# A Conformer convolution in a four-module trunk: the filters' tap products queued behind the norm's root, the gate kept in PSUM, and TensorE's filters half a tile later

## The chip, the cores and the metric

The kernel runs on one core of one Trainium2 chip. A core has five engines, each with its own instruction queue that is worked through in order: TensorE (PE; its weight loads are listed as PEld), VectorE (DVE), ScalarE (ACT), GpSimd (POOL) and SyncE (SP), which here issues nearly all DMAs. Engines wait for each other by semaphores. TensorE writes its products to PSUM, eight banks of 128 x 512 fp32; everything else lies in SBUF. The metric is the device time of one execution in microseconds (us), as a median of runs.

## What is computed

The trunk has two layers; each is a half-step SwiGLU FFN, a mixer, a second half-step FFN and a gated per-layer embedding, each behind an RMS norm. The mixer of layer 0 is the Conformer convolution, that of layer 1 a sparse attention. The change touches the convolution and the last norm.

```python
def rms_norm(x, g):
    return x * lax.rsqrt(jnp.mean(x * x, axis=-1, keepdims=True) + RMS_EPS) * g

def conformer_conv(h, w_pw1, b_pw1, w_dw, b_dw, ln_g, ln_b, w_pw2, b_pw2):
    u = h @ w_pw1 + b_pw1
    a, g = jnp.split(u, 2, axis=-1)
    u = a * jax.nn.sigmoid(g)
    u = lax.conv_general_dilated(u, w_dw[:, None, :], window_strides=(1,),
        padding=[(CONV_KERNEL - 1, 0)], feature_group_count=D_MODEL, ...) + b_dw
    mu = jnp.mean(u, axis=-1, keepdims=True)
    var = jnp.mean(jnp.square(u - mu), axis=-1, keepdims=True)
    u = jax.nn.silu((u - mu) * lax.rsqrt(var + LN_EPS) * ln_g + ln_b)
    return u @ w_pw2 + b_pw2

for i in range(DEPTH):                      # DEPTH = 2
    x = x + 0.5 * swiglu(rms_norm(x, ffn1_norm[i]), ...)
    h = rms_norm(x, mix_norm[i])
    x = x + (conformer_conv(h, ...) if i == 0 else nsa_mixer(h, ...))
    x = x + 0.5 * swiglu(rms_norm(x, ffn2_norm[i]), ...)
    x = x + jax.nn.sigmoid(rms_norm(x, ple_norm[i]) @ ple_w_gate[i]) * (p[i] @ ple_w_in[i])
return rms_norm(x, final_norm)
```

There are 512 tokens of 1024 channels; the filter has 31 taps and runs over each channel by itself.

## The kernel before

The activations lie transposed: eight tiles of 128 channels by 512 tokens. A weight block is 128 x 128, and eight blocks make a unit of 128 x 1024. SP loads a unit (`raw`), ACT copies it to a rounded half (`wh`, L230), and VectorE or GpSimd subtracts to get the rest (`wl`, L231). There are two `raw` buffers and five of `wh` and of `wl`, so a split waits until TensorE has done with the unit five before it. Each product is three matmuls, high by high, high by low, low by high (`mm3`, L254 to L256), of 512 columns.

An RMS norm's factor is not waited for. The products run on unnormalized activations; meanwhile TensorE sums squares over channels (L338), VectorE adds epsilon (`v`, L387), GpSimd takes the root (`r`, L331), TensorE spreads it over the partitions by four transposes (L363), and ACT copies it to `R` (L370). VectorE multiplies each product by `R` as it takes it out of PSUM.

The convolution (`conv`) goes over tiles c = 0 to 7. For each tile TensorE makes two groups of 24 matmuls: `pa` for the value, then `pg` for the gate. `glu` multiplies the gate by `R` (L538), has ACT take the sigmoid (L539), multiplies the value by `R` (L540) and multiplies both (L544, or L550 where the filter isn't TensorE's). The filter of tile 0 runs on ACT and GpSimd (L578, L579), those of tiles 1 and 2 on VectorE (62 steps over two PSUM banks, L563 and L565), those of tiles 3 to 7 on TensorE. For these:

- `taps` (L528) has GpSimd multiply the tap weights `dw`, a small load on SP, by a mask: four products `tw` of 128 x 1152 for each tile. The loop asks for them two tiles ahead (`TAPS_AT`), and there are buffers for two tiles.
- the gated tile goes to DRAM and comes back in another order (`ud` and `uu`, L545 and L546 on SP),
- TensorE runs 36 small matmuls over `uu` and `tw` (`dw_pe`, L636), ACT takes the result out (L641), and two more DMAs (`yd`, L642 and L643) bring it to its final order.

Where TensorE's filters stand between the groups is written out by hand. `PE_LATE` names the filters that run two tiles behind, after `pa` of the later tile; the others run after the loop. `centre` (L604 and after) forms a mean from the first four filtered tiles. Then come the products of the per-layer embedding, 16 "z tiles" of 6 matmuls each (`z_tiles`, ACT takes them out at L474), which fill TensorE while the layer norm is worked out; `FILL` says how many stand where: the last entry ahead of the remaining filters, the first ahead of the sums over all tiles (L722), the next two ahead of the second root's transposes, the rest behind them. Then VectorE and ACT normalize the tiles (L741 to L745) and TensorE multiplies them by `w_pw2`.

The last stage (`final`) works in two halves of 256 tokens. The last three tiles of the embedding's gate (`late`) run for half 0, then for half 1: product, times `R` (L1222), sigmoid (L1223), times z (L1224), add (L1225), square (L1227). `norm` has two steps for each half: sums and root, then transposes, ACT's copy (L1197), eight scalings on VectorE and GpSimd (L1206, L1204) and the output DMAs (L1208). `NORM_AT` places the two steps of half 0 at the second and third tile of half 1.

A scheduler orders what the code issues on each engine by its own estimate of time, within what the data and buffers allow, so an engine's order isn't simply that of the code.

## Time and profile before

| | |
|---|---|
| median of 3 runs (lowest to highest) | 2115.72 us (2115.25 to 2117.07) |
| the profiled execution's own time | 2116.84 us |
| its span in the profile | 2115.1 us |
| the convolution's groups, filters and z tiles | about 371 to 553 us |
| mean granted clock of TensorE over the span | 0.99 |

The profile shows one execution. A row of the timeline gives start, length, engine, line, operation, tile written and tiles read, and in brackets how long the engine stood idle just before and what ended that. `x8` means that eight like instructions are merged in the row. A row of the waits gives who waited for whom, the sum in us, how often, and the longest. PEclk is the share of full speed that TensorE was granted.

### The profile page before, as it was taken

The page shows a single profiled execution, that of the slowest core. Times are in us where ns is not written, and L with a number is a line of the kernel's source. Part 1 is how long each engine was busy: PE and PEld are TensorE (multiplying, and loading weights), DVE is VectorE, ACT ScalarE, POOL GpSimd, SP SyncE. Part 2 cuts the span into 40 slices and gives each one's busy share as a digit, 9 for nine tenths or more (in the row PEclk, how much of TensorE's full clock was granted, in tenths as well). Part 3 has the DMA queues.
Part 4 walks back from the last instruction along what each step waited for, and adds up shares of the span by engine and source line. Part 5 has one row for each costly group of instructions (what it writes and reads, how often), then busy time and mean ns, then how long its engine had stood idle before and what let it go on. Part 6 is the DMA issues. An engine that isn't in the chain of part 4 may idle for free. (4 is left out here: it accounts for less than half of the span.)

```text
span 2115.1 us, 25526 instructions
## 1 busy us (share of the span) xinstructions
PE 2067.5 (98%) x9608; PEld 1715.7 (81%) x9608; DVE 966.9 (46%) x1744; ACT 830.1 (39%) x1394; POOL 1030.9 (49%) x646
## 2 busy tenths in 40 slices
PE   9999999899999999999999999999999999999997
PEld 7888888688788888888788888888888778888887
DVE  5330334497635303335532133346989753213334
ACT  5322224552624222234432223326888642222333
POOL 2444443675435444444444444556666444444442
PEclk9999999999999999999999999999999999999998
DMA  5323323233463232233223322453232033223322
GB/s 171 94 96 100 100 93 100 69 127 105 154 183 126 98 100 94 96 100 115 93 98 100 99 92 98 156 174 116 83 91 95 33 123 98 93 99 100 96 94 75
DMA packets 77323, 223.30 MB, mean 106 GB/s; under 512 B 8624, under 2 KB 16592, under 8 KB 77200
## 3 DMA queue, kind: packets, MB, share of 16 engines
q1 hardware_dynamic: 76208, 219.26, 32.5%
q0 software_dynamic: 848, 2.34, 0.3%
q8 instruction: 76, 1.25, 0.2%
q14 instruction: 47, 0.39, 0.1%
q10 hardware_dynamic: 144, 0.07, 0.0%
HBM read 203.25 MB, written 16.29 MB: 104 GB/s over the span
## 5 line engine op out<-in xcount | busy, mean ns | idle before, releaser
L231 POOL TENSOR_TENSOR wl<-raw,wh 128x1024 fp32r<-128x1024 f32 x311 | 778.1, 2503 | 866.4 <-ACT wh L230 862.3
L230 ACT ACTIVATE wh<-raw 128x1024 fp32r<-128x1024 f32 (+1 forms) x331 | 348.9, 1056 | 932.9 <-PE b L255 833.3
L254 PE MATMUL b<-s,wh 128*128 128x512 f32 x1728 | 676.0, 392 | 4.8 <-ACT s L308 3.5
L255 PE MATMUL b<-s,wh 128*128 128x512 f32 x1728 | 674.6, 390 | 1.9 <-DVE s L309 1.6
L256 PE MATMUL b<-s,wl 128*128 128x512 f32 x1728 | 674.0, 390 | 0.0
L254 PEld LDWEIGHTS b<-s,wh 128*128 128x128 f32 x1728 | 325.4, 188 | 74.5 <-ACT s L308 5.7
L255 PEld LDWEIGHTS b<-s,wh 128*128 128x128 f32 x1728 | 325.3, 188 | 70.1 <-DVE s L309 3.0
L256 PEld LDWEIGHTS b<-s,wl 128*128 128x128 f32 x1728 | 325.1, 188 | 67.5
L254 PE MATMUL b<-hid,wh 128*128 128x512 f32 x704 | 273.9, 389 | 0.0
L256 PE MATMUL b<-hid,wl 128*128 128x512 f32 x704 | 273.2, 389 | 0.0
L255 PE MATMUL b<-hid,wh 128*128 128x512 f32 x704 | 273.2, 389 | 0.0
L411 DVE TENSOR_TENSOR t<-b,R 128x512 f32<-128x512 f32 x88 | 60.7, 690 | 348.2 <-PE b L256 348.2
L415 DVE TENSOR_TENSOR hid<-t,hid 128x512 fp32r<-128x512 f32 x88 | 173.2, 1970 | 55.4 <-ACT hid L414 55.2
L451 DVE SCALAR_TENSOR_TENSOR s<-b,s 128x512 f32<-128x512 f32 x64 | 44.3, 692 | 326.5 <-PE b L256 326.5
L254 PEld LDWEIGHTS b<-hid,wh 128*128 128x128 f32 x704 | 132.1, 188 | 27.6
L255 PEld LDWEIGHTS b<-hid,wh 128*128 128x128 f32 x704 | 132.1, 188 | 27.4
L256 PEld LDWEIGHTS b<-hid,wl 128*128 128x128 f32 x704 | 132.1, 188 | 27.4
L409 DVE TENSOR_TENSOR t<-b,R 128x512 f32<-128x512 f32 x88 | 60.7, 690 | 158.0 <-PE b L256 94.6
L1032 POOL TENSOR_SCALAR e<-e,sm,gates 128x512 f32<-128x512 f32 (+3 forms) x96 | 61.1, 642 | 40.8 <-DVE sm L1026 35.1
L414 ACT ACTIVATE hid<-t 128x512 fp32r<-128x512 f32 x88 | 55.4, 631 | 54.0 <-DVE t L412 54.0
L412 DVE TENSOR_TENSOR t<-t,t 128x512 f32<-128x512 f32 x88 | 68.5, 782 | 8.0 <-ACT t L410 0.2
L308 ACT ACTIVATE s<-s,small 128x512 fp32r<-128x512 f32 x48 | 38.0, 798 | 76.5 <-DVE s L451 34.5
(223 smaller groups left out, 2265.8 us busy)
## 6 DMA issues: line engine op xcount, KB each, us to landing
raw<-in_w SPq DMA_DIRECT2D x335, 512.0 KB, 3.5
skew<-table SPq DMA_DIRECT2D x16, 320.0 KB, 9.6
z<-t SPq DMA_DIRECT2D x16, 256.0 KB, 2.3
z<-z SPq DMA_DIRECT2D x16, 256.0 KB, 3.4
tt<-skew SPq DMA_DIRECT2D x16, 256.0 KB, 2.8
wr<-in_w SPq DMA_DIRECT2D x8, 512.0 KB, 3.8
q<-t SPq DMA_DIRECT2D x32, 128.0 KB, 2.4
s<-in_xT SPq DMA_DIRECT2D x8, 256.0 KB, 5.5
```

The lines of the kernel that those rows point to most:

```text
L230: self.nc.scalar.activation(h[:, c], t[:, c], AF.Copy)
L231: eng.tensor_tensor(l[:, c], t[:, c], h[:, c].bitcast(F32), op=OP.subtract)
L254: mm(out, sh, mh, start=start, stop=False)
L255: mm(out, sh, ml, start=False, stop=False)
L256: mm(out, sl, mh, start=False, stop=stop)
L409: nc.vector.tensor_tensor(gr, pg, R, op=OP.mult)
L411: nc.vector.tensor_tensor(ur, pu, R, op=OP.mult)
L412: nc.vector.tensor_tensor(ur, ur, gr, op=OP.mult)
L414: nc.scalar.activation(h, ur, AF.Copy)
L415: nc.vector.tensor_tensor(l, ur, h.bitcast(F32), op=OP.subtract)
L451: nc.vector.scalar_tensor_tensor(self.xs[m], p, 0.5, self.xs[m], op0=OP.mult, op1=OP.add)
L1032: nc.gpsimd.tensor_scalar(dst, dst, sm[:, a, bi:bi + 1], gate, op0=OP.mult, op1=OP.mult)
```

## The change

```diff
-PE_LATE = (3, 4, 5, 6)
+PE_LATE = (3, 4, 5)
...
-FILL = (6, 0, 4, 0)
+FILL = (6, 0, 4, 3)
...
     def rsqrt(self, v, n):
         y = self.tiny.tile([128, 4], F32, name="r", tag="r")[:, :n]
-        self.nc.gpsimd.tensor_tensor(y, v, self.power[:, :n], op=OP.pow)
+        self.root = self.nc.gpsimd.tensor_tensor(y, v, self.power[:, :n], op=OP.pow).ins
         return y
...
     def glu(self, c, pa, pg):
         nc, R = self.nc, self.R
-        tg, ta = self.tmp(), self.tmp()
+        tg, ta = pg, self.tmp()
...
         for c in range(KD):
             for t in TAPS_AT.get(c, ()):
-                self.T[t] = self.taps(t)
+                with self.tc.issue_after(self.root):
+                    self.T[t] = self.taps(t)
...
-                if p is pa and c - 2 in PE_LATE:
+                if p is pg and c - 2 in PE_LATE:
                     drain(queues["pe"].pop(0))
...
-                if h == 1 and m - late[0] in NORM_AT:
+                if h == 1 and m == late[1]:
                     next(norms[0])
```

The tap products may be issued only behind the latest root. `glu` multiplies the gate by `R` within its PSUM bank, ACT's sigmoid works there too, and L544 or L550 reads it there, so that the bank is held until then. The filters of tiles 3, 4 and 5 run after `pg` instead of `pa` of the tile two later; filter 6 runs right behind filter 5, and three z tiles stand ahead of filter 7. In the last stage only the first step of half 0's norm stands within half 1; the second follows behind all of half 1's tiles. Behind line 675 the changed kernel's line numbers are higher by one.

GpSimd's queue at the start of the convolution, a piece of the difference (- before, + changed; rows that differ in buffer numbers alone count as different):

```order
+L543 MEMSET uu_3072 128x4x8
+L331 TENSOR_TENSOR r<-v,power 128x4
 L528 TENSOR_TENSOR tw_2639<-bd,dw_2637 128x1152
 L528 TENSOR_TENSOR tw_2641<-bd,dw_2637 128x1152
 L528 TENSOR_TENSOR tw_2643<-bd,dw_2637 128x1152
 L528 TENSOR_TENSOR tw_2645<-bd,dw_2637 128x1152
-L528 TENSOR_TENSOR tw_2752<-bd,dw_2750 128x1152
-L528 TENSOR_TENSOR tw_2754<-bd,dw_2750 128x1152
-L528 TENSOR_TENSOR tw_2756<-bd,dw_2750 128x1152
-L528 TENSOR_TENSOR tw_2758<-bd,dw_2750 128x1152
-L331 TENSOR_TENSOR r<-v,power 128x4
-L579 TENSOR_TENSOR y_2694<-y_2694,t_2696 128x512
```

The root moved from behind the eight tap products of tiles 3 and 4 to ahead of them.

TensorE behind the last group of tile 7 (`b_3395` before, `b_3388` changed), first before, where L636 of `b_3557` is filter 6 and of `b_3598` filter 7:

```order
L256 MATMUL b_3395<-s_2549,wl_3188 128x512
L604 MATMUL b_3520<-sum_3170,meanr 128x512
L338 MATMUL b_3524<-meanr,sum_3170 128x1 x4
L636 MATMUL b_3557<-uu_3388,tw_2974 128x128 x9
L636 MATMUL b_3557<-uu_3388,tw_2976 128x128 x9
L636 MATMUL b_3557<-uu_3388,tw_2978 128x128 x9
L636 MATMUL b_3557<-uu_3388,tw_2980 128x128 x9
L636 MATMUL b_3598<-uu_3512,tw_3085 128x128 x9
```

and changed, where `b_3454` is filter 5, `b_3510` filter 6 and `b_3590` the first z tile:

```order
L256 MATMUL b_3388<-s_2549,wl_3142 128x512
L636 MATMUL b_3454<-uu_3230,tw_2860 128x128 x9
L636 MATMUL b_3454<-uu_3230,tw_2862 128x128 x9
L636 MATMUL b_3454<-uu_3230,tw_2864 128x128 x9
L636 MATMUL b_3454<-uu_3230,tw_2866 128x128 x9
L636 MATMUL b_3510<-uu_3381,tw_2970 128x128 x9
L636 MATMUL b_3510<-uu_3381,tw_2972 128x128 x9
L636 MATMUL b_3510<-uu_3381,tw_2974 128x128 x9
L636 MATMUL b_3510<-uu_3381,tw_2976 128x128 x9
L604 MATMUL b_3553<-sum_3124,meanr 128x512
L338 MATMUL b_3557<-meanr,sum_3124 128x1 x4
L254 MATMUL b_3590<-zp_3237,wh_3262 128x512
```

Filter 5 moved from ahead of tile 7's gate group to behind it, filter 6 ahead of the centre, and z tiles (three) to between the centre and filter 7. Further on, GpSimd's order has three weight differences (L231) between the last sum of squares (L623) and the second root, where it had two.

VectorE near the end of the program, where `t` and `s` are tile 7 of half 1, the `hid` rows scale half 0 for the output, and the second `v` is half 1's; before:

```order
L1192 TENSOR_SCALAR v<-b_16099 128x2
L1222 TENSOR_TENSOR t_16168<-b_16119,R 128x256
L1206 SCALAR_TENSOR_TENSOR hid_16149<-s_12199,small,b_16144 128x256
L1206 SCALAR_TENSOR_TENSOR hid_16154<-s_12203,small,b_16144 128x256
L1206 SCALAR_TENSOR_TENSOR hid_16154<-s_12205,small,b_16144 128x256
L1206 SCALAR_TENSOR_TENSOR hid_16158<-s_12209,small,b_16144 128x256
L1206 SCALAR_TENSOR_TENSOR hid_16163<-s_12211,small,b_16144 128x256
L1224 TENSOR_TENSOR t_16168<-t_16168,z_15941 128x256
L1225 TENSOR_TENSOR s_12213<-s_12213,t_16168 128x256
L1192 TENSOR_SCALAR v<-b_16175 128x2
```

and changed:

```order
L1193 TENSOR_SCALAR v<-b_16091 128x2
L1223 TENSOR_TENSOR t_16136<-b_16111,R 128x256
L1225 TENSOR_TENSOR t_16136<-t_16136,z_15933 128x256
L1226 TENSOR_TENSOR s_12205<-s_12205,t_16136 128x256
L1207 SCALAR_TENSOR_TENSOR hid_16148<-s_12191,small,b_16143 128x256
L1207 SCALAR_TENSOR_TENSOR hid_16153<-s_12195,small,b_16143 128x256
L1207 SCALAR_TENSOR_TENSOR hid_16153<-s_12197,small,b_16143 128x256
L1207 SCALAR_TENSOR_TENSOR hid_16157<-s_12201,small,b_16143 128x256
L1207 SCALAR_TENSOR_TENSOR hid_16162<-s_12203,small,b_16143 128x256
L1193 TENSOR_SCALAR v<-b_16167 128x2
```

The multiplication by z and the addition of tile 7 moved ahead of the five scalings of half 0.

## The prediction

> **What bounds the kernel now.** First the head of the page, then TensorE's own waits inside the convolution (355 to 640 us).

> ```profile
> span 2115.1 us, 25526 instructions
> PE 2067.5 (98%) x9608; PEld 1715.7 (81%) x9608; DVE 966.9 (46%) x1744; ACT 830.1 (39%) x1394; POOL 1030.9 (49%) x646
> ...
> PE b L363 <- POOL r L331: 11.1, 2, 9.6
> PE b L636 <- DMA uu<-ud: 7.2, 2, 3.9
> ```

> TensorE is busy for 98% of the span, and the change keeps every one of its matmuls. So only time in which it stands, or runs at a reduced clock, can go or come. In the convolution it stands four times, 18.3 us together. The timeline around the longest of them, with GpSimd first, then TensorE, and a row of the table of windows (its last columns are granted clock, DMA share, GB/s):

> ```profile
> 377.97 19.66 POOL L528 TENSOR_TENSOR tw<-bd,dw 128x1152 f32<-128x1152 f32 x8 [9.96 <-DMA dw<-in_dw]
> 397.59 1.04 POOL L331 TENSOR_TENSOR r<-v,power 128x4 f32<-128x4 f32 x1
> ...
> 380.64 0.16 DVE L387 TENSOR_SCALAR v<-b 128x4 f32<-128x4 f32 x1 [4.93 <-PE b L338]
> ...
> 386.23 0.39 PE L254 MATMUL b<-s,wh 128*128 128x512 f32 x1
> ...
> 388.72 0.39 PE L256 MATMUL b<-s,wl 128*128 128x512 f32 x1
> 398.68 1.12 PE L363 MATMUL b<-ident,r 128*128 128x128 f32 x4 [9.57 <-POOL r L331]
> ...
> 403.38 0.39 PE L254 MATMUL b<-s,wh 128*128 128x512 f32 x1
> ...
> 399.00:403.30 4.30, 4.30 (x13) 3.53 (x12) 2.09 (x3) 2.60 (x3) 0.00 (x0) 0.50 0.02 5
> ```

> The root's input v is there at 380.80, but eight tap products stand ahead of the root on GpSimd until 397.6; TensorE waits 9.57 us for it and then runs at a clock of 0.50 until 403.3. Its pace before is 0.227 us a product (386.23 to 388.72 in 11 steps).

> **The change, part by part.** The sum starts from the profiled execution's own time, 2116.84 us (its span and 1.74 around it), which is 1.1 above the median of the runs, 2115.72.

> *Root ahead of the taps.* With v at 380.80 and 1.04 for the root, r is ready at 381.9, while TensorE comes to the transposes at 388.95. The wait, 9.57, goes. Between 398.68 and 403.38 TensorE did four transposes and nine products; at full clock that is 0.65 (the row at 544.53 below) and 9 x 0.227 = 2.04, so 2.0 of those 4.7 us go too. **-11.6.** What moves behind the root: eight taps of 2.46 end at 401.6 instead of 397.6. Their first reader is filter 3, beyond 430 in any case, and GpSimd's own sums of tile 0 began only at 406.11 before. On SP the tap weights of tiles 5 and 6 wait for a free dw tile and hold the raw loads behind them some 4 us longer; the unit behind the second is loaded from about 402 and first used by tile 5's products at about 428: 26 us of cover.

> *Filters half a tile later.* The other long waits:

> ```profile
> 448.92 10.95 PE L636 MATMUL b<-uu,tw 128*128 128x128 f32 x72 [3.90 <-DMA uu<-ud]
> ...
> 470.64 8.20 PE L636 MATMUL b<-uu,tw 128*128 128x128 f32 x72
> ...
> 508.20 18.12 PE L636 MATMUL b<-uu,tw 128*128 128x128 f32 x144 [3.33 <-DMA uu<-ud]
> ```

> An undisturbed filter takes 8.20. Filter 3 waits 3.90 and runs 2.75 long behind it: -6.65. Filters 6 and 7 wait 3.33 and run 18.12 - 16.40 = 1.72 long: -5.05. **-11.7**, if VectorE has the gated tiles ready when the new order asks for them; that is the hard part.

> *Is VectorE ready?* The first rows are its groups between 400 and 508 us (busy, mean ns); the next two, from its timeline, bound a stretch in which it never idles; the last is a row at which GpSimd had nothing to do.

> ```profile
> L565 DVE SCALAR_TENSOR_TENSOR b<-u,dwc,b 128x512 f32<-128x512 f32 x58 | 40.0, 744 | 0.0
> L231 DVE TENSOR_TENSOR wl<-raw,wh 128x1024 fp32r<-128x1024 f32 x12 | 19.2, 1602 | 3.2 <-ACT wh L230 3.2
> L544 DVE SCALAR_TENSOR_TENSOR t<-t,small,t 128x512 f32<-128x512 f32 x5 | 11.4, 2288 | 0.4 <-ACT t L539 0.4
> ...
> L550 DVE SCALAR_TENSOR_TENSOR u<-t,small,t 128x512 f32<-128x512 f32 x3 | 5.2, 1749 | 2.4 <-ACT t L539 2.4
> L593 DVE SCALAR_TENSOR_TENSOR sum<-y,small,sum 128x512 f32<-128x512 f32 x3 | 4.6, 1548 | 0.0
> ...
> 416.26 1.41 DVE L563 TENSOR_SCALAR b<-u,dwc 128x512 f32<-128x512 f32 x2
> ...
> 500.64 2.61 DVE L544 SCALAR_TENSOR_TENSOR t<-t,small,t 128x512 f32<-128x512 f32 x1
> ...
> 523.74 0.75 DVE L593 SCALAR_TENSOR_TENSOR sum<-y,small,sum 128x512 f32<-128x512 f32 x1 [6.53 <-DMA y<-yd]
> ```

> L565 has one tensor in SBUF and one in PSUM and takes 744 ns each time, GpSimd busy or not. L544 and L593 have two in SBUF: 0.75 us with GpSimd idle (523.74), 2288 and 1548 ns on average beside it. With the gate in PSUM, L544 becomes L565's form. No row shows it as changed: the bounds are 0.74 and 2.29, and I take 0.74, the row of its own form. L538 writing PSUM and ACT's sigmoid there I price at nothing between 0 and 0.06 a piece (744 against L538's 682 ns).

> Before, the stretch to the end of tile 6's L544 is 503.25 - 416.26 = 87.0. In the new order one L565 (0.7), one L231 (1.6) and one L593 (1.5) stand behind that L544 instead of ahead; four L544 shrink by 1.54 (6.2), one L550 by about 1.1. That leaves 75.9. It starts some 10.3 earlier: R comes 9.7 earlier, one copy of 1.1 less stands ahead of tile 1's sigmoid on ACT, and one more L231 ahead of the stretch takes half of that back. So tile 6's gated tile is done at 406.0 + 75.9 = 481.9, and the filter can start 4.95 later as before (503.25 to 508.20, two DMAs): **486.9**. TensorE: transposes until 389.6, 13 groups of 24 products (13 x 5.45 = 70.8), three filters (24.6): **485.0**. Filter 6 waits about 1.9; I add no reduced clock, because the 1.57 us wait at 544.53 below was followed by none. **+1.9**, with bounds 0 and 12: if L544 gains nothing, it is 7.3 + 1.9, and 2.75 of reduced clock as behind filter 3. Filters 3, 4 and 5 have 6, 10 and 13 us in hand by the same ledger. Filter 7 has three z tiles and the centre as cover.

> [...]

> *End of the convolution.* Three z tiles (6 products, 1.36 each, 4.1 together) now run ahead of filter 7 instead of behind the second root.

> ```profile
> 539.97 1.06 ACT L230 ACTIVATE wh<-raw 128x1024 fp32r<-128x1024 f32 x1 [1.46 <-PE b L255]
> ...
> 541.11 2.40 POOL L231 TENSOR_TENSOR wl<-raw,wh 128x1024 fp32r<-128x1024 f32 x1 [5.33 <-ACT wh L230]
> 543.45 1.03 POOL L331 TENSOR_TENSOR r<-v,power 128x4 f32<-128x4 f32 x1
> ...
> 544.53 0.65 PE L363 MATMUL b<-ident,r 128*128 128x128 f32 x4 [1.57 <-POOL r L331]
> 553.43 0.86 PE L254 MATMUL b<-tw,wh 128*128 128x512 f32 x3
> ...
> 550.01 0.68 DVE L745 TENSOR_TENSOR tw<-y,tw 128x512 fp32r<-128x512 f32 x1
> ```

> Before, L363 to the first product of w_pw2 is 8.90, filled by six z tiles. Now three tiles fill 4.1, and TensorE waits for the first normalized tile, ready 6.16 after L363 (550.69 - 544.53): 8.90 - 6.16 = 2.74 is got back of the 4.1 moved, +1.3. And the new order puts one more L231 ahead of the root on GpSimd; its split waits for z tile 12's products, with one z tile (1.36) between it and L363 instead of two: from release to root 4.51, less 1.36, is a wait of 3.2 for 1.57, +1.6. **+2.9**, bounds 0 and 5.

> *The last stage.*

> ```profile
> 2100.55 0.41 ACT L1223 ACTIVATE t<-t 128x256 f32<-128x256 f32 x1
> 2100.68 2.04 DVE L1206 SCALAR_TENSOR_TENSOR hid<-s,small,b 128x256 f32<-128x256 f32 x5 [0.21 <-ACT hid L1197]
> ...
> 2102.65 0.46 DVE L1224 TENSOR_TENSOR t<-t,z 128x256 f32<-128x256 f32 x1
> 2103.14 0.42 DVE L1225 TENSOR_TENSOR s<-s,t 128x256 f32<-128x256 f32 x1
> 2103.60 0.42 ACT L1227 ACTIVATE hid<-s 128x256 f32<-128x256 f32 x1 [2.64 <-DVE s L1225]
> ...
> 2106.47 0.16 DVE L1192 TENSOR_SCALAR v<-b 128x2 f32<-128x2 f32 x1 [2.90 <-PE b L338]
> ```

> L1224 waits on VectorE behind five L1206 of the first half. Put ahead of them, it starts at 2101.0, not 2102.65. But the five now stand ahead of the last v: sigmoid's end 2100.96, then L1224, L1225, the square, the ACT copy (0.4) and 2.04 give 2104.9 for 2106.47. **-1.55**, bounds 0 and -2.2.

> Sum: -11.6 - 11.7 + 1.9 + 2.9 - 1.55 = -20.05; 2116.84 - 20.05 = **2096.8**.

> **The rivals.** (a) *VectorE stays the bound.* L544 keeps waiting for GpSimd: filter 6 waits 9.2 and runs 2.75 long, 10.0 more than forecast: 2106.8. For it: GpSimd is still busy nearly throughout, and the 1602 ns of L231 shows the same waiting. Against it: 58 rows of L565 at one duration. (b) *Nothing waits*: filter 6 and the root's second wait are covered, -3.5: 2093.3. For it: VectorE's other rows on two SBUF tensors meet GpSimd by chance, and 2 us of luck in 76 suffice. Against it: the forecast already prices them at their mean. (c) *Slower, by the banks.* The gate now holds its PSUM bank from the product to L544. Tile 6's first group takes the bank of tile 4's gate, tile 5's gate group that of tile 3. My ledger frees them at 442.8 and 427.2 for 447.0 and 433.4: 4 and 6 us of room. If VectorE runs over 10 us later than that, TensorE stands about 6 us for three banks (these two and the accumulator's that filter 4 takes), each with 2.75 of reduced clock: +26.3, or 2123. It decides from a lag of 4 us and turns the sign at about 10. (d) *The move does nothing*: excluded, since the built order shows the root ahead of the taps and v is there.

> A wait of 3.2 us at the second root may cost clock. After 3.33 (filter 6) the trace has 1.7 us of loss, after 1.57 none; here such a loss would mostly lie under the wait for the first normalized tile (0.7 left over).

> [...]

> **How the numbers follow.** Forecast 2096.8: 0.62, own range 2093 to 2101. (b) 0.14, (a) 0.17, (c) 0.03; 0.04 for a loss that I do not see, half of it eating the whole gain. The range takes in the bounds: all at their best, 2116.84 - 23.3 - 2.2 = 2091.3, and 1.1 less on the median's scale, so 2090; (a) with 0.7 of lost clock at the second root gives 2107.5, so 2108. A measurement of this kernel can tell about 0.2% (4.2 us) from no change: faster by more than that 0.94, within it 0.03, slower 0.03.

> **What would show it.** L363 near 389 without a wait and a clock of 1.00 behind it; L544 at about 0.74 us; filter 3 without a wait, filter 6 waiting 0 to 4; the second L363 waiting about 3; L1224 ahead of L1206 at the end. Wrong if L544 stays above 1.5, if TensorE's waits name VectorE ahead of a product group (c), or if the gain before 510 us is given back by 560.

## The result and the profile after

| | before | changed |
|---|---|---|
| median (lowest to highest, 4 runs each) | 2115.70 us (2115.25 to 2117.07) | 2095.92 us (2094.80 to 2097.39) |
| ratio, 95% interval | | 0.9906 (0.9889 to 0.9923) |
| span of the profiled execution | 2115.1 us | 2094.1 us |

The kernel became 19.8 us faster; 2096.8 had been forecast, 18.9 faster. Four stretches make up the 20.95 us between the two spans. The middle two are divided at the start of `v` of the first root (L387) and at the start of the first product of `w_pw2` (the first L254 that reads `tw`):

| stretch | before | changed | difference |
|---|---|---|---|
| up to `v` of the first root | 380.64 | 381.91 | +1.27 |
| from there to the first product of `w_pw2` | 172.79 | 151.52 | -21.27 |
| from there to the last copy of `R` (L370) | 1516.99 | 1517.94 | +0.95 |
| from there to the end | 44.64 | 42.72 | -1.92 |

The change doesn't touch the first and the third: over the 14 profiles of this case, all shown below, the first runs from 380.4 to 383.1 and the third from 1516.5 to 1518.9. So the second and the fourth are what to read. Here are the changed kernel's head of the page and TensorE's waits from 370 to 540 us. Before, the convolution had 18.3 us of waits in four places:

```profile
span 2094.1 us, 25510 instructions
...
PE 2060.0 (98%) x9608; PEld 1709.4 (82%) x9608; DVE 956.3 (46%) x1744; ACT 830.6 (40%) x1394; POOL 1031.2 (49%) x646
...
PE b L363 <- POOL r L331: 2.9, 1, 2.9
PE b L636 <- DMA uu<-ud: 1.1, 1, 1.1
PE b L255 <- DVE tw L746: 0.4, 1, 0.4
```

4.4 us of waiting are left. The first root in the timeline, and the granted clock behind the transposes in the table of windows (fifth figure, behind the count):

```profile
381.91 0.16 DVE L387 TENSOR_SCALAR v<-b 128x4 f32<-128x4 f32 x1 [4.93 <-PE b L338]
382.16 1.04 POOL L331 TENSOR_TENSOR r<-v,power 128x4 f32<-128x4 f32 x1 [12.89 <-DVE v L387]
383.19 8.30 POOL L528 TENSOR_TENSOR tw<-bd,dw 128x1152 f32<-128x1152 f32 x3
...
390.22 0.60 PE L363 MATMUL b<-ident,r 128*128 128x128 f32 x4
...
390.82:395.32 4.50, 4.50 (x21) 1.00 0.29 110
```

The root runs first and is ready seven microseconds before TensorE asks for it; L363 has no bracket, and the clock stays at 1.00. Now the filters on TensorE, tile 6's L544, and VectorE's groups from 385 us to the end of that L544:

```profile
439.67 8.20 PE L636 MATMUL b<-uu,tw 128*128 128x128 f32 x72
...
481.18 0.73 DVE L544 SCALAR_TENSOR_TENSOR t<-t,small,b 128x512 f32<-128x512 f32 x1
486.87 8.28 PE L636 MATMUL b<-uu,tw 128*128 128x128 f32 x72 [1.12 <-DMA uu<-ud]
500.95 8.20 PE L636 MATMUL b<-uu,tw 128*128 128x128 f32 x72
...
L231 DVE TENSOR_TENSOR wl<-raw,wh 128x1024 fp32r<-128x1024 f32 x14 | 22.3, 1596 | 12.8 <-ACT wh L230 12.6
...
L463 DVE TENSOR_TENSOR zp<-t,zp 128x512 fp32r<-128x512 f32 x4 | 4.4, 1089 | 0.0
...
L550 DVE SCALAR_TENSOR_TENSOR u<-t,small,b 128x512 f32<-128x512 f32 x3 | 3.4, 1139 | 0.1
L544 DVE SCALAR_TENSOR_TENSOR t<-t,small,b 128x512 f32<-128x512 f32 x4 | 2.9, 736 | 0.0
...
L588 DVE TENSOR_SCALAR sum<-y,small 128x512 f32<-128x512 f32 x1 | 0.6, 600 | 0.0
```

Filter 3 doesn't wait, filter 6 waits 1.12, and each takes its undisturbed 8.2 (8.28 behind a wait). L544 takes 736 ns on average, where it took 2288. The end of the convolution and of the program:

```profile
525.34 2.35 POOL L231 TENSOR_TENSOR wl<-raw,wh 128x1024 fp32r<-128x1024 f32 x1 [2.93 <-DMA raw<-in_w]
527.65 1.02 POOL L331 TENSOR_TENSOR r<-v,power 128x4 f32<-128x4 f32 x1
528.72 0.65 PE L363 MATMUL b<-ident,r 128*128 128x128 f32 x4 [2.92 <-POOL r L331]
531.57 0.62 ACT L745 ACTIVATE tw<-y 128x512 fp32r<-128x512 f32 x1
533.43 1.10 PE L254 MATMUL b<-tw,wh 128*128 128x512 f32 x4
...
2081.46 0.42 ACT L1224 ACTIVATE t<-t 128x256 f32<-128x256 f32 x1 [2.87 <-DVE t L1223]
2081.91 0.43 DVE L1225 TENSOR_TENSOR t<-t,z 128x256 f32<-128x256 f32 x1 [0.48 <-ACT t L1224]
...
2083.55 2.05 DVE L1207 SCALAR_TENSOR_TENSOR hid<-s,small,b 128x256 f32<-128x256 f32 x5 [0.76 <-ACT hid L1198]
2085.51 0.15 DVE L1193 TENSOR_SCALAR v<-b 128x2 f32<-128x2 f32 x1
```

The second root stands behind the added L231 and TensorE waits 2.92 for it. In the last stage the multiplication by z follows the sigmoid at once, and the last `v` comes 3.63 us behind the sigmoid's end, 5.51 before.

### The profile page after: what moved, and what is told of

Same layout as the page of the kernel before. It is cut to its first block, busy times and chain, and to the rows that moved or that the text cites. A ratio compares the mean times of both kernels' runs of the same rounds, so it can differ in the third digit from the quotient of the medians.

```text
span 2094.1 us, 25510 instructions
## 1 busy us (share of the span) xinstructions
PE 2060.0 (98%) x9608; PEld 1709.4 (82%) x9608; DVE 956.3 (46%) x1744; ACT 830.6 (40%) x1394; POOL 1031.2 (49%) x646
## 5 line engine op out<-in xcount | busy, mean ns | idle before, releaser
L231 POOL TENSOR_TENSOR wl<-raw,wh 128x1024 fp32r<-128x1024 f32 x311 | 777.5, 2501 | 858.1 <-ACT wh L230 840.4
L230 ACT ACTIVATE wh<-raw 128x1024 fp32r<-128x1024 f32 (+1 forms) x331 | 348.8, 1056 | 920.5 <-PE b L255 819.1
L254 PE MATMUL b<-s,wh 128*128 128x512 f32 x1728 | 675.3, 392 | 6.6 <-ACT s L308 5.8
L255 PE MATMUL b<-s,wh 128*128 128x512 f32 x1728 | 673.7, 390 | 1.5 <-DVE s L309 1.2
L256 PE MATMUL b<-s,wl 128*128 128x512 f32 x1728 | 673.8, 390 | 0.0
L254 PEld LDWEIGHTS b<-s,wh 128*128 128x128 f32 x1728 | 325.1, 188 | 75.4 <-ACT s L308 7.5
L255 PEld LDWEIGHTS b<-s,wh 128*128 128x128 f32 x1728 | 324.8, 188 | 69.6 <-DVE s L309 2.6
L256 PEld LDWEIGHTS b<-s,wl 128*128 128x128 f32 x1728 | 324.8, 188 | 67.7
L254 PE MATMUL b<-hid,wh 128*128 128x512 f32 x704 | 273.9, 389 | 0.0
L256 PE MATMUL b<-hid,wl 128*128 128x512 f32 x704 | 273.2, 389 | 0.0
L255 PE MATMUL b<-hid,wh 128*128 128x512 f32 x704 | 273.2, 389 | 0.0
L256 PEld LDWEIGHTS b<-hid,wl 128*128 128x128 f32 x704 | 132.1, 188 | 27.5
L255 PEld LDWEIGHTS b<-hid,wh 128*128 128x128 f32 x704 | 132.1, 188 | 27.5
L254 PEld LDWEIGHTS b<-hid,wh 128*128 128x128 f32 x704 | 132.1, 188 | 27.3
```

Source lines behind the costliest of these rows:

```text
L230: self.nc.scalar.activation(h[:, c], t[:, c], AF.Copy)
L231: eng.tensor_tensor(l[:, c], t[:, c], h[:, c].bitcast(F32), op=OP.subtract)
L254: mm(out, sh, mh, start=start, stop=False)
L255: mm(out, sh, ml, start=False, stop=False)
L256: mm(out, sl, mh, start=False, stop=stop)
```

## The experiments

The parts were put into the kernel before one by one, and taken out of the changed kernel one by one. The table reads each profile in four numbers: when tile 6's L544 ends ("gated": the gated tile is ready), when filter 6 starts, how long TensorE waited for it, and when the first product of `w_pw2` starts. The three times are counted from the start of `v` of the first root, and the last of them is called the stretch. It is a sharper measure than whole runs, which differ by 2 us: the changed kernel gave 151.52 and 151.56 in two profiles. But it is one profile, and another kernel below gave 148.19 and 151.63, as half clock followed a wait at filter 7 in one of the two (2.52 us) and not in the other (0.71). So a difference of two or three microseconds in it is sure only where its parts are seen in the rows. A ratio is to the kernel before on the same chip; "place" is the filters' place with its z tiles. The last four rows have the changed last stage too, 1.92 us that lie outside the stretch.

| parts in the kernel | tile 6 gated | filter 6 starts | its wait | first of `w_pw2` | ratio (95%) |
|---|---|---|---|---|---|
| none (before) | 122.61 | 127.56 | 3.33 | 172.79 | 1 |
| root | 106.66 | 113.36 | 4.00 | 160.31 | 0.9944 (0.9928 to 0.9961) |
| gate | 117.93 | 123.95 | 4.65 | 170.12 | 0.9979 (0.9970 to 0.9989) |
| place | 117.47 | 122.24 | 5.71 | 171.57 | 0.9992 (0.9983 to 1.0002) |
| gate, place | 110.87 | 115.81 | 0.17 | 163.87 | 0.9943 (0.9928 to 0.9958) |
| root, place | 105.21 | 110.16 | 5.29 | 159.28 | 0.9934 (0.9919 to 0.9949) |
| root, gate | 105.12 | 111.09 | 4.59 | 156.18 | 0.9915 (0.9900 to 0.9930) |
| all (changed) | 100.00 | 104.96 | 1.12 | 151.52 | 0.9906 (0.9889 to 0.9923) |

### One part alone

Root:

```diff
             for t in TAPS_AT.get(c, ()):
-                self.T[t] = self.taps(t)
+                with self.tc.issue_after(self.root):
+                    self.T[t] = self.taps(t)
```

> The kernel before with the tap products queued behind the root, and nothing else of the change. Theory A (VectorE sets when the filters of tiles 3 and 6 can start, so of TensorE's gain only what VectorE also gains is kept): TensorE loses its 9.57 us wait at L363 and the 2.0 us of half clock, VectorE's stretch starts about 9.9 us earlier; filter 3 then waits 5.6 us instead of 3.90 and filter 6 also longer; the whole is worth -9.9 us, 2105.8. Rival B (the terms add up, the filters' waits stay as they are): -11.6 us, 2104.1. What tells them apart is filter 3's wait at L636: 5.6 by A, 3.9 by B.

12.5 us less in the stretch; 0.9944 is 11.8 us of 2115.7, so rival B's sum fits. But filter 3 waited 2.82, less than either theory said: with the root early VectorE's L544 took 1736 ns on average for 2288 (tile 6's, with no row of GpSimd beside it, 0.74 us for 2.61), so VectorE gained more than the root's 9.7 us: tile 6 is gated 16.0 us earlier. Theory A's 5.6 us is refuted.

Gate:

```diff
-        tg, ta = self.tmp(), self.tmp()
+        tg, ta = pg, self.tmp()
```

> The kernel before with the gate kept in PSUM, and nothing else of the change. Theory A (VectorE sets the filters' start, and L544 falls from 2.29 to 0.74 us): tile 3's gated tile comes 2.6 us earlier and filter 3 waits 1.3 us without half clock, tile 6's comes 7.3 us earlier and filter 6 waits 1.3 us; the whole is worth -9.0 us, 2106.7. Rival B (the place of the filters is what took their waits away, the gate alone gives nothing): L544 at 0.74 but waits of 3.9 and 3.3 us kept, 2115.7. Rival C (an exchange of GpSimd's time: L544 falls, other operations of VectorE on two SBUF tensors rise as much): 2115.7, L231 and L593 longer by some 7 us in sum.

L544 fell to 739 ns as all three said, but the stretch lost 2.7 us, not 9. Filter 3 waited 1.04 without half clock, near theory A's 1.3. Tile 6 came 4.7 us earlier and not 7.3, for L231 rose from 1602 to 1774 ns on average over the same 12: a part of rival C. Then its way through DRAM took 6.0 us for 5.0. TensorE, which no longer lost time at filter 3, stood ready for filter 6 4.9 us earlier, so it waited 4.65 there, and 2.7 us of half clock followed.

Place:

```diff
-PE_LATE = (3, 4, 5, 6)
+PE_LATE = (3, 4, 5)
-FILL = (6, 0, 4, 0)
+FILL = (6, 0, 4, 3)
...
-                if p is pa and c - 2 in PE_LATE:
+                if p is pg and c - 2 in PE_LATE:
```

> The kernel before with TensorE's filters half a tile later and three z tiles ahead of filter 7 (PE_LATE, FILL, pg for pa), and nothing else of the change. Theory A (VectorE sets filter 6's start): filter 3's wait and half clock go (-6.65), but filter 6 then waits some 8 us with 2.75 us of half clock; the whole is worth about 0 (+0.3), 2116. Rival B (the place takes the waits away by itself, as the term of the forecast is written): -6.65 to -11.7 us, 2104 to 2109, filter 6 waiting 0 to 3 us.

Theory A: 1.2 us in the stretch, and a ratio that can't be told from 1. Filter 3's 6.65 us went but for a wait of 0.57. Most of it came back: filter 6 waited 5.71 with half clock behind it, 3.5 us more than filters 6 and 7 cost before, and the second root's wait grew by 1.35.

### One part undone

The same lines, taken back in the changed kernel. Place:

> The changed kernel with the filters back at their former places (PE_LATE, FILL and pa as before); root, gate and last stage as changed. Theory A: VectorE's stretch is early and short, so filter 3 waits about 3.0 us and filter 6 about 1.4 us, and only VectorE's date for filter 6 counts: 2095.1, the same as the changed kernel within 2 us. Rival B (the place is worth its term of -11.7, or at least -6.65): 2102.5 to 2107.6.

Neither: 0.9915 of before is 2097.7 us on the forecast's scale, which the whole runs can't tell from the changed kernel's (0.9906 and, below, 0.9894), but the stretch is 4.7 us longer. The time at which VectorE has tile 6 ready does count (filter 6 waits 4.59), but the place moves that time: tile 6 is gated at 105.1 instead of 100.0, and its way through DRAM takes 1 us more. From `v` to that L544 VectorE is idle as long as in the changed kernel (14.5 us) and busy 5.1 us longer: L463 takes 7.0 us for 4.4, the same 14 L231 take 24.3 for 22.4, and one L565 and one L593 more stand ahead. Theory A had assumed a time that doesn't depend on the place.

Gate:

> The changed kernel with the gate back in SBUF; root, filters' place and last stage as changed. Theory A (rival (a) of the forecast: L544 takes 2.29 us again, tile 6's gated tile is 7.3 us later): filter 6 waits 8 to 9 us and half clock follows, +10.0 us, 2105.9. Theory D (L544 is long only where it meets an instruction of GpSimd, and the filters' new place moves the tap products of GpSimd away from it, so L544 stays near the 1.05 us of the run with the place alone): tile 6 is 2 to 4 us later, filter 6 waits 3 to 5 us, with 1 to 2.7 us of half clock: 2098.5 to 2102. No effect of the gate at all would be 2095.9.

7.8 us more in the stretch; 0.9934 is 2101.7 us. Filter 6 and its clock on TensorE, then VectorE's groups from 385 us to the end of tile 6's L544, at 487 here:

```profile
491.98 10.88 PE L636 MATMUL b<-uu,tw 128*128 128x128 f32 x72 [5.29 <-DMA uu<-ud]
...
493.50:495.00 1.50, 1.50 (x9) 0.50 0.87 306
...
L231 DVE TENSOR_TENSOR wl<-raw,wh 128x1024 fp32r<-128x1024 f32 x14 | 22.9, 1639 | 11.1 <-ACT wh L230 11.0
L463 DVE TENSOR_TENSOR zp<-t,zp 128x512 fp32r<-128x512 f32 x4 | 6.9, 1735 | 0.0
L550 DVE SCALAR_TENSOR_TENSOR u<-t,small,t 128x512 f32<-128x512 f32 x3 | 5.3, 1781 | 0.2 <-ACT t L539 0.2
...
L544 DVE SCALAR_TENSOR_TENSOR t<-t,small,t 128x512 f32<-128x512 f32 x4 | 3.3, 834 | 0.0
...
L588 DVE TENSOR_SCALAR sum<-y,small 128x512 f32<-128x512 f32 x1 | 2.3, 2323 | 0.0
```

Theory D comes nearest: with the gate in SBUF L544 takes only 0.83 us on average here. The tap products follow a filter, whose buffers they take: before, one ran beside three of these four L544 (2.06 to 2.61 us each), with the place alone beside none (0.74 to 1.84 us). The time lies in D's range; the wait, 5.29, lies just above its 3 to 5, and 2.68 us of half clock follow. Tile 6 is gated 5.2 us later than in the changed kernel: VectorE is busy 7.3 us longer from `v` to its L544, and idle 2.1 us less. Of the 7.3, L544 is 0.4 and L550, which reads the gate too, 1.9; 4.3 are L463 and L588, and 0.7 is one more L565.

Root:

> The changed kernel without the order of the tap products (they may run ahead of the root again); gate, filters' place and last stage as changed. Theory A (the root's wait and half clock are 11.6 us of TensorE, and VectorE's early start is worth 10, so the order is worth nearly the same with and without the rest): from v to the first product of w_pw2 162 to 164 us instead of 151.5, the wait of 9.6 us at L363 back, filter 6 waiting 0 to 2 us; 2106 to 2108. Rival B (gate and place give only what they gave alone, 2.7 and 1.2 us, while the root is late): 168.9 us for that stretch, 2113.

163.87 us for the stretch, theory A. So the root is worth 12.4 us with the other two parts and 12.5 without, and gate and place gave 8.9 together, where alone they gave 2.7 and 1.2. About 1.5 us of this profile are chance (the last section shows the rows): here the second root's wait of 2.92 was followed by half clock, and 6.23 us lie between L363 and the first product of `w_pw2`, for 4.71 in the changed kernel after the same wait. Without them, by estimate, the root would be worth 10.8 with the other two, and gate and place together 10.4.

### Does GpSimd make VectorE's operations long?

The same L544 with the gate in SBUF, in the kernel before with GpSimd's row beside it, and with the place alone, where no row of GpSimd overlaps it:

```profile
491.83 10.87 POOL L528 TENSOR_TENSOR tw<-bd,dw 128x1152 f32<-128x1152 f32 x4 [7.52 <-PE b L636]
```

```profile
497.92 0.75 DVE L544 SCALAR_TENSOR_TENSOR t<-t,small,t 128x512 f32<-128x512 f32 x1 [0.25 <-ACT t L539]
```

Before, tile 6's L544 (500.64, shown in the prediction) took 2.61 beside the last of the four tap products, which end at 502.70; with the place alone it took 0.75. The test by itself takes nearly all of GpSimd's work in the convolution out of the run with the gate in SBUF:

```diff
-                with self.tc.issue_after(self.root):
-                    self.T[t] = self.taps(t)
+                if t == 3:
+                    with self.tc.issue_after(self.root):
+                        T3 = self.taps(t)
+                self.T[t] = T3
...
             nc.scalar.activation(self.rs(t), ...)
-            nc.gpsimd.tensor_tensor(y, y, t, op=OP.add)
             yield
```

> The run with the gate back in SBUF, with GpSimd's work in the convolution taken out: the filter of tile 0 adds nothing (L579 is left out), and the tap products are made for tile 3 alone and used for all of TensorE's filters, so the output is not the reference's. It is read for VectorE's durations between the first root and filter 6. Theory A (VectorE's operations on two SBUF tensors are long where they meet an instruction of GpSimd): the long ones go, L231 1.21 to 1.3 us each, L463 0.7, L593 and L544 0.75, L550 1.1; tile 6's gated tile comes 8 to 13 us earlier than 105.2 us behind v, filter 6 doesn't wait, and v to the first product of w_pw2 falls from 159.3 to 151 or less. Rival B (they are long for a cause on VectorE's own side, or by ScalarE's or DMA traffic): L231 keeps a mean of 1.6 and L463 of 1.7 us, and tile 6 comes within 3 us of 105.2.

Its groups on VectorE from 400 to 490 us, where L587 is the L588 of the others:

```profile
L565 DVE SCALAR_TENSOR_TENSOR b<-u,dwc,b 128x512 f32<-128x512 f32 x58 | 40.1, 743 | 0.0
L231 DVE TENSOR_TENSOR wl<-raw,wh 128x1024 fp32r<-128x1024 f32 x12 | 14.6, 1216 | 6.8 <-ACT wh L230 6.8
...
L463 DVE TENSOR_TENSOR zp<-t,zp 128x512 fp32r<-128x512 f32 x4 | 2.6, 673 | 0.0
...
L587 DVE TENSOR_SCALAR sum<-y,small 128x512 f32<-128x512 f32 x1 | 0.5, 469 | 0.0
```

Shown: L231 falls to 1216 ns, from 1576 in the run with the gate in SBUF (400 to 486 us), and L463 from 1735 to 673, while L565, with one tensor in PSUM, stays at 743. ScalarE's copies and nearly all DMAs were still there. Tile 6 is gated at 93.3 instead of 105.2 and filter 6 doesn't wait. The stretch is 151.61, not under 151: the wait of 2.92 at the second root is still there, and here too half clock followed it, so that 6.17 us lie between that L363 and the first product of `w_pw2` for 4.71. So in these rows operations on two SBUF tensors were long beside GpSimd (L544 2.61 us beside a tap product and 0.75 without), while the 58 rows of L565 took 739 to 752 ns before, GpSimd busy or not, and 743 on average with it quiet. Not every row beside GpSimd was long: in the changed kernel one L463 took 0.68 us beside a sum of L579 (466.25). And L588, which reads one SBUF tensor, was long too: it took 469 ns with GpSimd quiet, 2323 in the run with the gate in SBUF, and with the place alone 2.29 us (467.15) beside a tap product that starts 0.12 us ahead of it.

### The z tiles

Three z tiles stand ahead of filter 7 in the changed kernel. Three more kernels put them elsewhere, to fill the waits that are left: the first puts all ahead of the second root's transposes, the second puts one ahead of filter 6 and the other two ahead of those transposes, the third leaves one at filter 7, with one ahead of filter 6 and one ahead of the transposes. The first needs a number alone, the others also move a line; the second was run twice, the third has (6, 0, 5, 1):

```diff
-FILL = (6, 0, 4, 3)
+FILL = (6, 0, 7, 0)
```

```diff
-FILL = (6, 0, 4, 3)
+FILL = (6, 0, 6, 0)
...
             if CONV_ON[c - 1] == "pe" and c - 1 not in PE_LATE:
+                fill = itertools.chain(*[self.z_tiles(i, ZP[i]) for i in range(L)])
+                next(fill)
                 drain(queues["pe"].pop(0))
...
-        fill = itertools.chain(*[self.z_tiles(i, ZP[i]) for i in range(L)])
```

> The changed kernel once more, as the reference on the chip of the three runs beside it. Every theory: 0.9906 of before (0.9889 to 0.9923); from v of the first root to the first product of w_pw2 151.5 us as in its first profile, with a wait of about 1.1 us at filter 6 and 2.9 us at the second L363.

The changed kernel again, for comparison: 2095.44 us, 0.9894 (0.9880 to 0.9909), stretch 151.56, waits of 1.22 and 2.92.

> The changed kernel with the three z tiles that stand ahead of filter 7 moved to ahead of the second root's transposes (FILL = 6, 0, 7, 0). Theory A: filter 7's input is there 1.4 us before TensorE comes to it without them (tile 7's gated tile at 490.2, and 5 us for two DMAs, against 496.7), so it still doesn't wait; the wait of 2.92 us for the second root goes, since v to L363 is covered by three more z tiles (4.1 us): -2.9 us, 2093.0. Rival B (the z tiles ahead of filter 7 are needed, as the third part of filter 7's two DMAs lies under them): filter 7 waits 2 to 4 us with or without half clock, and the whole is 0 to +2.

Rival B: 2097.06, 0.9903 (0.9888 to 0.9918), stretch 152.79. The second root's wait went, but filter 7 waited 2.43 and ran 1.7 us long. `uu` of tile 7 takes 9.2 us from its L544, not 5: on its queue two weight loads of 512 KB (487.89) and filter 5's output (489.70) stand ahead of `ud` (490.92).

> As the run with FILL = (6, 0, 7, 0), with one of the seven z tiles put ahead of filter 6. Theory A (VectorE's date for filter 6 is fixed, TensorE waits 1.12 us for it): one z tile of 1.4 us covers that wait, and six are still enough ahead of the transposes: -4.0 us against the changed kernel, 2091.9, and 1.1 below the run beside it. Rival B (TensorE's earlier or later arrival moves what VectorE meets on GpSimd, so filter 6's wait is luck): anything within 2 us of the run beside it.

2093.96, 0.9890 (0.9873 to 0.9906), stretch 148.19: theory A in this profile.

> The run with one z tile ahead of filter 6 and six ahead of the second root's transposes, once more, for its time. Theory A (3.4 us less from v to the first product of w_pw2 than the changed kernel, and nothing given back): 148.2 us for that stretch again, 0.989 of before or a little less, 2092 on the scale of the changed kernel's 2095.9. Rival B (the 3.4 us are given back behind the convolution): 0.990 to 0.991.

2096.39, 0.9893 (0.9877 to 0.9910), stretch 151.63: of the same kernel. Now filter 7 waited 2.52 with half clock, where it had waited 0.71: the first DMA of tile 7 took 6.0 us for 4.1. So 148.19 was one of two outcomes, and a gain isn't shown.

> The changed kernel with one z tile ahead of filter 6, one ahead of filter 7 and five ahead of the second root's transposes (FILL = 6, 0, 5, 1). Theory A (filter 6 lacks 1.1 us, the two DMAs of filter 7 take between 0.7 and 2.5 us longer than TensorE can wait from one execution to the next, so one z tile of 1.4 us leaves 0 to 1.2 us without half clock; and with one difference L231 less ahead of the root five z tiles cover it): from v of the first root to the first product of w_pw2 147.5 to 149 us for 151.5, about 0.988 of before, 2092 on the scale of the changed kernel's 2095.9. Rival B (the z tile among the filters puts one more transfer on the DMA queue, and filter 7 comes as much later as the tile covers): filter 7 waits 2 us or more with half clock, 150 to 152 us.

2094.11, 0.9891 (0.9874 to 0.9907). Filter 7 and the second root on TensorE:

```profile
500.82 8.28 PE L636 MATMUL b<-uu,tw 128*128 128x128 f32 x72 [1.23 <-DVE y L616]
...
526.98 0.60 PE L363 MATMUL b<-ident,r 128*128 128x128 f32 x4
```

Theory A in this one profile: 1.23 us at filter 7 without half clock, none at the root, and a stretch of 148.59, 2.9 us under the changed kernel's. Its whole time can't be told from the changed kernel's 0.9894 and 0.9906: 2.9 us is 0.14%, less than the width of any of these intervals.

## Why the prediction was right, and where not

**Root ahead of the taps, -11.6.** Right. L363 comes 8.31 us behind `v` for 18.04, and the clock stays up. By the profiles it is worth 12.5 alone and 10.8 to 12.4 with the other parts. What goes beyond 11.6 when it is alone is VectorE's, where tile 6's L544 took 0.74 us for 2.61.

**Filters half a tile later, -11.7.** Filter 3's 6.65 and the 5.05 of filters 6 and 7 went as counted (filter 6's 1.12 belongs to the next term). But the step booked them under the place, with a clause "if VectorE has the gated tiles ready", and that clause is the content: the place alone is worth 1.2. Gate and place each bring tile 6 about 5 us forward, both 11.7 (122.61 to 110.87). Where the wait for filter 6 stayed at 4 us or more (4.00 to 5.71), 1.6 to 2.9 us of half clock still followed (five rows of the table). And the place puts some 3 us of work behind filter 6: the centre (1.67), which stood ahead of it and lay under its wait, and the longer wait for the second root (1.35), which has fewer z tiles ahead of it. So each alone gives little, and both 8.9.

**Is VectorE ready, +1.9.** The number held: tile 6 was gated 74.5 us after the start of the stretch that never idled (forecast 75.9), and the wait was 1.12. In part that is luck, for its main term had the wrong reason. "Four L544 shrink by 1.54" came true (9.1 to 2.9 us in sum), but in the new place they would be nearly as short with the gate in SBUF (3.3). The gate's 7.8 us there are 2.3 in L544 and L550, 4.3 in L463 and L588 (6.9 and 2.3 us without the gate, 4.4 and 0.6 with it, 2.6 and 0.5 with GpSimd quiet), and half clock (2.7 without the gate, none with it). L463, 7.4 us before and 4.4 changed, is not in the forecast's sum at all. Rival (a) named the price, 10.0, nearly right (7.8) for a state of L544 that didn't occur.

**End of the convolution, +2.9.** Mis-sized: +1.3. The second root's wait grew by 1.35 (forecast 1.6). The 4.1 us of z tiles moved were got back in full, not 2.74 of them: L363 to `w_pw2` takes 4.71 and not 6.16. The forecast made the first product wait for the whole normalized tile, its low half too; the first four products need only the rounded half, there at 532.19, and the low half (L746) cost 0.41. Behind the wait of 2.92 no clock was lost in the changed kernel's two profiles. That is luck too: after the same wait 1.5 us were lost with the root late and with GpSimd quiet, and they did not lie under the wait for the normalized tile, as the forecast thought they mostly would.

**Last stage, -1.55.** -1.92, shown by four profiles with the old order (44.64 to 44.70 us from the last copy of `R` to the end) and ten with the new (42.65 to 42.94). It wasn't run alone.

By these sizes the sum is -11.6 - 11.7 + 1.1 + 1.3 - 1.92 = -22.82, where the profiles have -23.2 in the two stretches and the forecast had -20.05; 2.2 of it was taken back in the profiled pair by the two stretches that the change doesn't touch. So it is in part luck that the whole time came out closer to the forecast than the terms did. Of the rivals, (b) failed by the 1.12 and 2.92 that stayed, and (c) didn't occur: no group of the convolution waits for VectorE between 370 and 540. The one wait for VectorE there is the 0.41 of `w_pw2`.

## What to carry to other kernels

Where the time at which one engine is ready sets another's start, two edits that each bring that time forward can be worth little alone and much together: here the gate gave 2.7 us, the place 1.2 and both 8.9, as with each alone a wait of 4.65 or 5.71 us for filter 6 stayed and 2.7 or 2.9 us were lost to half clock behind it. So test edits in pairs before one is dropped. An operation's mean duration beside another engine need not belong to its form: tile 6's L544 took 2.61 us before and, in the same form, 0.75 with the place alone. Before pricing a shorter form, look which rows of the other engine it overlaps, and what will overlap it after the move. And where a loss hangs on how a wait happens to fall, as the clock does here (0 or 1.5 us lost behind the same wait of 2.92), profile a kernel twice before a difference of its size is read.

## What the runs showed of the hardware

**Half clock behind a short wait.** In the kernel before, the granted clock was 0.50 inside the convolution from 393.04 to 403.28 us, from 447.66 to 454.48 and from 509.10 to 512.51, so for 10.24, 6.83 and 3.41 us, and these starts lie 16 and 18 times 3.41 us apart. The rows of windows below are such steps of 3.41 us (TensorE's busy time, its instructions, the clock). First filter 7 and its wait of 2.43 us in the run with FILL = (6, 0, 7, 0), then the wait of 2.92 us at the second root with the root late, and the same wait in the changed kernel, where it ends at 528.72:

```profile
499.13 9.90 PE L636 MATMUL b<-uu,tw 128*128 128x128 f32 x72 [2.43 <-DMA uu<-ud]
...
496.40:499.81 3.41, 0.98 (x9) 1.00 0.61 190
499.81:503.22 3.41, 3.41 (x19) 0.50 0.29 79
```

```profile
538.02 0.65 PE L363 MATMUL b<-ident,r 128*128 128x128 f32 x4 [2.92 <-POOL r L331]
...
535.79:539.20 3.41, 1.18 (x7) 1.00 0.70 252
539.20:542.61 3.41, 3.41 (x9) 0.50 0.16 61
```

```profile
523.78:527.19 3.41, 2.02 (x9) 1.00 0.79 281
527.19:530.60 3.41, 1.88 (x10) 1.00 0.73 238
530.60:534.01 3.41, 3.41 (x16) 1.00 0.16 59
```

**A weight load beside a small transfer.** SP's queue for tile 6, with the root alone, and in the changed kernel:

```profile
487.77 0.33 SPq L207 DMA_DIRECT2D raw<-in_w  x1
488.43 0.32 SPq L545 DMA_DIRECT2D ud<-t  x1
492.38 0.37 SPq L546 DMA_DIRECT2D uu<-ud  x1
```

```profile
481.94 0.32 SPq L545 DMA_DIRECT2D ud<-t  x1
484.00 0.37 SPq L546 DMA_DIRECT2D uu<-ud  x1
```

`uu` is issued when `ud` has landed: 3.95 us behind it where a 512 KB load was issued 0.66 us ahead, 2.06 where none was. A smaller extra stands in the runs with the gate alone (3.03) and with root and gate (3.02), with a load 1.3 us ahead; with a load 2.5 us ahead, in the kernel before, there is none (2.07). The load wasn't moved by itself, so its part in it is read from these rows and not tested.
